# Two float16 parts for a decoder block's output and mixing products, and its scales worked out apart

## The chip, the cores and the metric

The kernel runs on one core of one Trainium2 chip. The metric is the device time of one execution in microseconds (us); lower is better. Engines are named as the profile names them: PE is TensorE (PEld its weight loads), DVE is VectorE, ACT is ScalarE, POOL is GpSimd, SP is SyncE, which issues most DMAs.

## What is computed

One decoder block on 1024 tokens of width 1024. Two token mixers work side by side on the normed input: dilated attention in three groups of eight heads, whose outputs are merged per head with softmax weights, and a causal convolution module. Their outputs are gated and added, mixed by a matrix, normed and added to the input; a SwiGLU feed-forward follows. The part that the change touches:

```python
o = jnp.einsum('gbsh,gbshd->bshd', alpha, jnp.stack(outs, axis=0))
y_attn = o.reshape(B, S, ATTN_OUT_W) @ w_attn_out              # 512 -> 1024
merged = jax.nn.sigmoid(z_ga) * y_attn + jax.nn.sigmoid(z_gc) * y_conv
x = x + rms_norm(merged @ w_mix_out, g_post_mix)               # 1024 -> 1024
h = rms_norm(x, g_pre_ffn)
x = x + rms_norm(swiglu_ffn(h, w_ffn_in, w_ffn_out), g_post_ffn)
```

## The kernel before, in words

**Products in parts.** Every large product keeps float32 accuracy with three matmuls: each operand is split into a high and a low part, and high x high, high x low and low x high are added up. Most stages use two float16 parts. Their operands are brought to a common size first by a power of two (a "scale": `peaks` or `early_scales` squares the weights on ACT with a running sum, `total` and `bound` (L142) spread the sum over the partitions by a small PE product with a block of ones (L146), and DVE makes the power of two and its inverse). Three stages use two float32r parts instead, which need no scale: the first one, the attention's output product, the mixing product (and the last, the FFN's second product).

**Order of work.** Python writes all engines' instructions in one order. `tick` (L250), called after each group of matmuls of the main loop, runs what is planned beside it: steps due at a given tick (`later`), pieces of weight splitting (one each `PIECE` ticks), and generators, of which one that yields k goes on k + 1 ticks later. Each engine then runs its own instructions in that order and waits only for data and for buffers. `slot` hands out 42 buffers of 128x1024 floats, `bank` PSUM banks by name: `g` for products, `s` (two) for small results, `t` (two) for transposes.

**The stages.** GLU (to about 190 us of the trace), gates (`gate_pair`, seven pairs, to 317), queries and keys (`qk_pair`, twelve pairs, to 530), values with the attention beside them and the rest of the attention, the convolution's output product (to 853), then

- the attention's output product (L1745 to L1759, 853 to 897): eight columns n, two halves each, and per half `unit` (L478), 4 x 3 matmuls of 128x512 (L485, L487, L489), 192 in all. DVE multiplies the result by the gate (L1753) and adds the other branch (L1754); ACT and DVE split it (L1756, L1759) into `mop`, the mixing product's operand;
- the mixing product (L1782 to L1809, 897 to 990): eight tiles of 128 tokens (the first two together), 48 matmuls of 128x512 each (L1794), 384 in all, two ticks after every six. After each tile a generator `mix_norm` (L1506) norms it; that of tile 3 and that of tile 7 also transpose four tiles' results, eight groups of four transposes (L1524) into the two `s` banks, from which ACT copies them (L1530) and splits them (L1399). It waits 9 ticks, then writes one group each 2 ticks. After a tile, L1807 runs all generators but the newest to their end at once;
- the FFN's two products (to the end), float16 in the first and float32r in the second (L2068).

**The merge** (L1319), a generator for each of four pairs of heads (its transposes start at 717 us in the first and end at 844 us in the fourth): DVE multiplies three outputs of 128x1024 by weights (L1347), adds them (L1349, L1352). Partition p holds the tokens 8p to 8p + 7, so eight 128x128 transposes (L1363, four to a bank) give every eighth token each, and ACT's copy (L1366) and DVE's low part (L1368, pairs 2 and 3 alone) put them in order with a stride. Pairs 0 and 1 go out to DRAM and come back later in `out_parts` (L1377).

**Weights of these products.** `part` (L309) splits each in two halves: ACT casts the high part (L320), DVE takes the low part of the first half and POOL that of the second (L321).

**Early scales.** `early_scales` (L191) is a generator started before the query and key pairs (L1666). For 20 weights (12 of the values, 8 of the convolution's output) it issues a load on SP (L212) and about 13 ticks later a Square on ACT with a sum (L208); after each group it works out the scale by `bound`. `input_scales` (L167) does so for two rows of gains at the start.

Of the kernel before, what the change touches and what calls it, by code (L numbers as in the profile page):

```python
# [18 lines left out]
T = 1024  # L19
# [52 lines left out]
class Build:  # L72
# [77 lines left out]

    def scales(self, i):
# [15 lines left out]
    def input_scales(self):  # L167
# [4 lines left out]
        for c in (C_PRE, C_PREF):  # L172
            m = self.tiny(2, "pk", 4)
            nc.scalar.activation(self.junk[:, :8], self.col8(c), AF.Square, scale=1 / H_TOP, accum_out=m[:, 0:1])
            p.append(self.total(m, 1))
        yield 6
        for e, c in enumerate((C_PRE, C_PREF)):
# [3 lines left out]
            self.bound(t[:, 0:1], p[e])  # L181
# [9 lines left out]
    def early_scales(self, groups):  # L191

        nc = self.nc
        m = self.small.tile([128, 24], F32, name="em")
        t = self.small.tile([128, 5], F32, name="cs")
        self.conv_bias = self.small.tile([128, 8], F32, name="cb")
        for c, x, k in ((0, C_GLN, 32), (1, C_BLN, 1)):
            nc.scalar.activation(self.junk[:, :8], self.col8(x), AF.Square, scale=k * A_TOP, accum_out=m[:, c:c + 1])
        pa = self.total(m[:, 0:2], 2)
        yield 6  # L200
        self.bound(t[:, 0:1], pa)
        nc.vector.reciprocal(t[:, 1:2], t[:, 0:1])
        yield 2
        todo = [(e, j) for e, jobs in enumerate(groups) for j in jobs]
        x, ends = None, {len(jobs) + 2 + sum(len(y) for y in groups[:e]): e for e, jobs in enumerate(groups)}
        for n in range(2, len(todo) + 3):
            if x is not None:
                nc.scalar.activation(self.junk, x, AF.Square, scale=W_TOP, accum_out=m[:, n - 1:n])  # L208
            x = None
            if n < len(todo) + 2:  # L210
                x = self.slot()
                nc.sync.dma_start(x, self.jobs[todo[n - 2][1]][0])  # L212
            yield 3
            if n in ends:
# [10 lines left out]
                for j in jobs:  # L225
                    self.scale[j] = tuple(u[:, i:i + 1] for i in range(1, 5))
            else:
                yield 8
        w = self.scale[groups[1][0]][0]
        nc.vector.tensor_tensor(t[:, 4:5], t[:, 0:1], u[:, 0:1], op=OP.mult)  # L230
        nc.vector.tensor_scalar(self.conv_bias, self.col8(C_BCO), t[:, 1:2], w, op0=OP.mult, op1=OP.mult)
        nc.vector.tensor_scalar(self.vun, self.scale[groups[0][0]][1], 1 / (KEEP * P_TOP), None, op0=OP.mult)
        self.act_scale, self.conv_un = t[:, 1:2], t[:, 4:5]
# [75 lines left out]
    def part(self, i, c):  # L309
# [7 lines left out]
        if i in self.f16:  # L317
# [1001 lines left out]
    def merge(self, hp, st, last):  # L1319
# [34 lines left out]
        yield 2 + 2 * late  # L1354
        if hp < 2:
            hi = self.slot()
        else:
            hi, lo = self.slot(F32R), self.slot(F32R)
# [825 lines left out]
```

## Time and profile before

| | us |
|---|---|
| median of 3 runs | 1618.56 (1618.04 to 1619.05) |
| the profiled execution | 1618.76 |
| its span, first to last instruction | 1616.9 |
| PE busy | 1592.5 (98%) |
| DVE busy | 1244.3 (77%) |
| ACT busy | 997.8 (62%) |
| POOL busy | 449.0 (28%) |

The granted TensorE clock is 0.999 of full speed over the span (2.4 GHz). A matmul's duration in the trace covers its whole way through the array, and the next one starts before it ends; what a stream of matmuls costs is read from the distance between starts. "Idle before" in a timeline row is the time in which the engine had nothing, and behind it stands what ended that.

### The profile page before, as it was taken

Reading aid. Unit: us, or ns where it says so; the run is one execution under the profiler, and the core shown is the slowest. Engines: PE = TensorE matmul, PEld = TensorE weight load, DVE = VectorE, ACT = ScalarE, POOL = GpSimd, SP = SyncE. Lnnn points to the kernel's source line nnn. Section 1 sums busy time; section 2 is a strip of 40 time slices with the busy share of each in tenths; the row PEclk is TensorE's granted clock in tenths of the full one; section 3 lists DMA queues with packets and bytes.
Section 4 is the critical chain, followed back from the end, with each engine's and each line's share of the span. In section 5 each row is a group of like instructions: output and inputs, shape, how many; then the busy total and the mean of one; then the engine's idle time right before and its main releaser. Section 6 shows DMA issues by size and latency. Waiting matters only on the chain.

```text
span 1616.9 us, 25346 instructions
## 1 busy us (share of the span) xinstructions
PE 1592.5 (98%) x9034; PEld 979.5 (61%) x9034; DVE 1244.3 (77%) x2415; ACT 997.8 (62%) x1900; POOL 449.0 (28%) x372
## 2 busy tenths in 40 slices
PE   8999999999999999999999999999999999999998
PEld 6744444444444799976657876444444444588886
DVE  6879999989899768787686655876656666677686
ACT  6476666778776578877752566654555454454453
POOL 0006777767777343654401200000000000000000
PEclk9999999999999999999999999999999999999999
DMA  4353333455666765777847432033322232594334
GB/s 175 109 204 110 111 135 145 145 183 201 199 180 141 223 189 159 178 224 225 253 154 278 173 115 91 27 143 111 124 99 98 108 128 91 205 335 121 134 105 156
DMA packets 158906, 254.02 MB, mean 157 GB/s; under 512 B 63313, under 2 KB 82444, under 8 KB 158780
## 3 DMA queue, kind: packets, MB, share of 16 engines
q1 hardware_dynamic: 154572, 240.23, 44.8%
q0 software_dynamic: 3920, 11.91, 2.3%
q8 instruction: 71, 1.16, 0.3%
q14 instruction: 55, 0.45, 0.1%
q10 hardware_dynamic: 288, 0.27, 0.0%
HBM read 178.52 MB, written 78.55 MB: 159 GB/s over the span
## 4 chain that ended last, share of the span: by engine, by line
PE 82%; DVE 9%; ACT 4%; issue 2%; POOL 2%; DMA 0%; DVEq 0%; SPq 0%; POOLq 0%; ACTq 0%
PE p L2068 13%; PE p L501 13%; PE p L503 13%; PE p L502 13%; PE p L485 4%; PE p L489 4%; PE p L487 4%; PE p L1794 3%; PE p L1142 2%; PE p L1144 2%; PE p L1146 2%; DVE p L885 2%; PE p L739 2%; PE p L1274 2%; PE p L1237 2%
## 5 line engine op out<-in xcount | busy, mean ns | idle before, releaser
L501 PE MATMUL p<-b,b 128*128 128x512 f16 x1032 | 390.9, 379 | 2.1 <-ACT c L515 1.6
L503 PE MATMUL p<-b,b 128*128 128x512 f16 x1032 | 391.1, 379 | 1.5 <-POOL b L340 1.5
L502 PE MATMUL p<-b,b 128*128 128x512 f16 x1032 | 391.0, 379 | 0.0
L2068 PE MATMUL p<-b,b 128*128 128x512 f32 x924 | 209.8, 389 | 0.0
L2068 PEld LDWEIGHTS p<-b,b 128*128 128x128 f32 x924 | 173.5, 188 | 36.1
L503 PEld LDWEIGHTS <-b 128*128 128x128 f16 x1032 | 100.8, 98 | 125.2 <-POOL b L340 4.0
L501 PEld LDWEIGHTS <-b 128*128 128x128 f16 x1032 | 100.9, 98 | 121.3
L502 PEld LDWEIGHTS <-b 128*128 128x128 f16 x1032 | 100.8, 98 | 119.3 <-issue 3.0
L885 DVE SCALAR_TENSOR_TENSOR p<-b,par,p 128x511 f32<-128x511 f32 (+14 forms) x232 | 164.1, 740 | 0.0
L485 PE MATMUL p<-b,b 128*128 128x512 f16 (+1 forms) x368 | 141.3, 384 | 1.6 <-ACT b L330 1.6
L489 PE MATMUL p<-b,b 128*128 128x512 f16 (+1 forms) x368 | 140.7, 382 | 0.4 <-DVE b L331 0.4
L487 PE MATMUL p<-b,b 128*128 128x512 f16 (+1 forms) x368 | 140.7, 382 | 0.0
L331 DVE SCALAR_TENSOR_TENSOR b<-d,sc,b 128x1024 f16<-128x1024 f32 x40 | 51.2, 1281 | 87.7 <-ACT b L330 87.7
L340 POOL TENSOR_TENSOR b<-d,b 128x1024 f16<-128x1024 f32 x44 | 93.9, 2134 | 83.7 <-ACT b L339 83.7
L1146 PE MATMUL p<-b,b 128*128 128x256 f16 x384 | 104.7, 273 | 0.0
L1144 PE MATMUL p<-b,b 128*128 128x256 f16 x384 | 104.7, 273 | 0.0
L1142 PE MATMUL p<-b,b 128*128 128x256 f16 x384 | 104.7, 273 | 0.0
L1399 ACT CAST b<-b 128x512 fp32r<-128x512 f32 (+1 forms) x117 | 72.1, 617 | 43.0 <-PE p L2068 18.5
L1400 DVE TENSOR_TENSOR b<-b,b 128x512 fp32r<-128x512 f32 (+1 forms) x117 | 80.1, 688 | 19.6 <-ACT b L1399 18.2
L1794 PE MATMUL p<-b,b 128*128 128x512 f32 x384 | 90.0, 392 | 0.0
L1251 ACT ACTIVATE c<-c,stat 128x128 f32<-128x128 f32 (+1 forms) x192 | 84.3, 443 | 6.8 <-DVE stat L1241 6.7
L515 ACT COPY c<-p 128x512 f32<-128x512 f32 x43 | 25.2, 585 | 100.2 <-PE p L503 64.6
(296 smaller groups left out, 3431.6 us busy)
## 6 DMA issues: line engine op xcount, KB each, us to landing
b<-w_in SPq DMA_DIRECT2D x30, 512.0 KB, 6.4
b<-w_v SPq DMA_DIRECT2D x24, 512.0 KB, 4.5
b<-w_fi SPq DMA_DIRECT2D x24, 512.0 KB, 4.4
d<-w_in SPq DMA_DIRECT2D x23, 512.0 KB, 4.3
dqS<-c SPq DMA_DIRECT2D x44, 256.0 KB, 2.0
b<-w_fo SPq DMA_DIRECT2D x44, 256.0 KB, 5.4
c<-dqS SPq DMA_DIRECT2D x44, 256.0 KB, 4.2
d<-w_fi SPq DMA_DIRECT2D x20, 512.0 KB, 3.5
```

The source lines that it names most:

```text
L485: nc.tensor.matmul(ps, hi[:, s], a, start=kt == 0, stop=False)
L487: nc.tensor.matmul(ps, hi[:, s], b, start=False, stop=False)
L489: nc.tensor.matmul(ps, lo[:, s], a, start=False, stop=kt == nk - 1)
L501: nc.tensor.matmul(ps, hi[:, s], a, start=first and kt == 0, stop=False, skip_group_check=True)
L502: nc.tensor.matmul(ps, hi[:, s], b, start=False, stop=False, skip_group_check=True)
L503: nc.tensor.matmul(ps, lo[:, s], a, start=False, stop=kt == 3, skip_group_check=True)
L885: nc.vector.scalar_tensor_tensor(A[i][:, j:], src[i][:, :H - j], w[i], A[i][:, j:], op0=OP.mult, op1=OP.add)
L1142: nc.tensor.matmul(o, a, hi[:, s], start=kt == 0, stop=False)
L1144: nc.tensor.matmul(o, a, lo[:, s], start=False, stop=False)
L1146: nc.tensor.matmul(o, b, hi[:, s], start=False, stop=kt == KT - 1)
L1794: nc.tensor.matmul(banks[tt][nh], st, wt[:, nh * H:(nh + 1) * H], start=bool(kt == 0 and a), stop=bool(kt == KT - 1 and b))
L2068: nc.tensor.matmul(acc[t], x, y, start=first and e == 0, stop=last and e == 2, skip_group_check=True)
```

## The change

- Output and mixing products get two float16 parts: `B.f16` takes in the jobs `ao` (8 weights of 512 columns) and `mx` (8 of 1024), `mop` is packed float16, and `both` gives float16 parts for pairs 0 and 1. Their scales come from `early_scales`, now for 36 weights (16 more loads and Squares), with one job each 12 ticks, started before the gate pairs.
- The size of the merged attention output is measured: one Square with a sum on ACT per merge, and a new generator `mix_scales` after the fourth.
- `root` takes the place of `bound` for gains and for that sum: a PE transpose of one column, spread to 128, and a DVE maximum along the row. `largest` prepares the gains' column. Small DVE operations that stood together are spread by yields.
- The merge's transposes: for each half of the partitions (64 rows), eight transposes of 64x128 into every eighth column of a bank, so 16 a merge, with the result in token order.
- The weights `ao` and the first two of `mx` are brought to size by ACT first (`pre`), and POOL takes all their low parts; the other six of `mx` go by `scaled_parts` (ACT and DVE).
- In the output product the high part of a half is taken one half later, the low part two halves later.
- `mix_norm` of tile 3 writes one group of transposes each 3 ticks.

The diff, cut to its core:

```diff
+    def root(self, a, m):
+        ps = self.bank(self.stag)
+        nc.tensor.transpose(ps[:, :128], m.to_broadcast([128, 128]), self.ident)
+        nc.vector.tensor_reduce(a, ps[:, :128], AX.X, OP.max)
...
     def early_scales(self, groups):
...
             if n < len(todo):
                 x = self.slot()
-                nc.sync.dma_start(x, self.jobs[todo[n - 2][1]][0])
+                src, k, _ = self.jobs[todo[n][1]]
+                nc.sync.dma_start(x[:, :k], src)
             yield 3
...
             else:
-                yield 8
+                yield 7
...
+    def mix_scales(self):
+        yield 4
+        nc.vector.tensor_reduce(r, self.osq[:, :4], AX.X, OP.add)
+        yield 4
+        self.root(on, r)
...
-        if i in self.f16:
+        if i in self.pre:
+            if c == 0:
+                nc.scalar.activation(r[:, :n], r[:, :n], AF.Copy, scale=self.scale[i][0])
+            nc.scalar.copy(hi[:, s], r[:, s])
+            nc.gpsimd.tensor_tensor(lo[:, s], r[:, s], hi[:, s], op=OP.subtract)
+        elif i in self.f16:
...
-        yield 2 + 2 * late
+        yield 2
+        nc.scalar.activation(self.junk, O[0], AF.Square, scale=self.o_scale, accum_out=self.osq[:, hp:hp + 1])
...
+        yield 1 + 2 * late
...
         for h in range(2):
             ps = self.bank("t")
-            for i in range(4):
-                u = h * 4 + i
-                nc.tensor.transpose(ps[:, i * 128:(i + 1) * 128], O[0][:, u * 128:(u + 1) * 128], self.ident)
+            r = slice(h * 64, h * 64 + 64)
+            for u in range(8):
+                nc.tensor.transpose(ps.rearrange("p (m u) -> p u m", u=8)[:, u], O[0][r, u * 128:(u + 1) * 128],
+                                    self.ident[r, r])
...
-            self.OT[hp] = self.both(x)
+            self.OT[hp] = self.both(x, self.o_scale, True)
...
-                yield 1
+                yield 1 + (tt == 3)
...
-    B.f16 = {*range(glu_jobs[3][0], ao[0]), *range(B.fi0, len(J))}
-    B.early = [i for p in vj.values() for i in p] + co
-    B.pre = {*range(glu_pairs[0] - 1, min(vj[0, 0]))}
+    B.f16 = {*range(glu_jobs[3][0], len(J))}
+    B.early = [i for p in vj.values() for i in p] + co + ao + mx
+    B.pre = {*range(glu_pairs[0] - 1, min(vj[0, 0])), *ao, *mx[:2]}
...
+    es = B.bg(B.early_scales((B.early[:12], co, ao, mx)))
     for n in range(4):
         B.gate_pair(B.d_ga[2 * n:2 * n + 2], ga[n])
...
-    es = B.bg(B.early_scales((B.early[:12], co)))
...
-            nc.vector.tensor_tensor(c[:, s], ps, c[:, s], op=OP.mult)
+            nc.vector.scalar_tensor_tensor(c[:, s], ps, B.att_un, c[:, s], op0=OP.mult, op1=OP.mult)
...
+            x = mop[hf][n] = B.packed()
+            todo.append((x, c[:, s]))
+            if len(todo) > 1:
+                high(*todo[-2])
+            if len(todo) > 2:
+                low(*todo.popleft())
```

## Rows read from the trace of the kernel before

**Rows 1.** The page: busy time of each engine, its share of the span, instructions.

```profile
PE 1592.5 (98%) x9034; PEld 979.5 (61%) x9034; DVE 1244.3 (77%) x2415; ACT 997.8 (62%) x1900; POOL 449.0 (28%) x372
```

**Rows 2.** Windows: length, busy time by engine, clock; gates, queries and keys, output product.

```profile
190.00:317.00 127.00, 126.70 (x593) 57.32 (x592) 121.38 (x199) 87.80 (x132) 94.99 (x62) 1.00 0.39 141
317.00:530.00 213.00, 212.25 (x996) 95.94 (x994) 187.32 (x347) 161.47 (x266) 158.01 (x101) 1.00 0.61 182
853.10:896.80 43.70, 43.70 (x194) 36.21 (x193) 34.17 (x53) 14.46 (x30) 7.08 (x8) 1.00 0.78 274
```

**Rows 3.** Waits of PE: who, for whom, us in total, times, longest.

```profile
PE p L1524 <- ACT b L1530: 1.4, 1, 1.4
PE p L1363 <- DVE c L1287: 0.9, 1, 0.9
```

**Rows 4.** Timeline of PE, output product (start, duration): first and last of 28 rows.

```profile
859.68 0.39 PE L487 MATMUL p<-b,b 128*128 128x512 f32 x1
...
865.80 0.39 PE L487 MATMUL p<-b,b 128*128 128x512 f32 x1
```

**Rows 5.** Timeline of PE, gate pairs: first and last of 48 rows.

```profile
299.82 0.38 PE L501 MATMUL p<-b,b 128*128 128x512 f16 x1
...
309.96 0.38 PE L503 MATMUL p<-b,b 128*128 128x512 f16 x1
```

**Rows 6.** Timeline of PE, mixing product, its sixth tile with the transposes of L1524.

```profile
960.91 1.64 PE L1794 MATMUL p<-b,b 128*128 128x512 f32 x6
962.39 0.60 PE L1524 MATMUL p<-ident,b 128*128 128x128 f32 x4
962.74 1.64 PE L1794 MATMUL p<-b,b 128*128 128x512 f32 x6
965.79 0.66 PE L1524 MATMUL p<-ident,b 128*128 128x128 f32 x4 [1.41 <-ACT b L1530]
```

**Rows 7.** Timeline of ACT in the same tile.

```profile
962.89 1.15 ACT L1516 ACTIVATE b<-d,rr 128x1024 f32<-128x1024 f32 x1 [0.87 <-DVE rr L1484]
...
965.07 0.68 ACT L1530 ACTIVATE b<-p,hg 128x512 f32<-128x512 f32 x1
```

**Rows 8.** Timeline of PE, a merge's transposes between two products.

```profile
721.15 0.60 PE L1363 MATMUL p<-ident,b 128*128 128x128 f32 x4
721.58 0.38 PE L485 MATMUL p<-b,b 128*128 128x512 f16 x1
```

**Rows 9.** Timeline of PE at the start: matmuls of one float32 column.

```profile
33.03 1.84 PE L582 MATMUL p<-mean_col,b 128*128 128x1 f32 x16
```

**Rows 10.** Weight loads by line: shortest, median, longest ns; first and last start.

```profile
L582 PEld LDWEIGHTS p<-mean_col,b x32: 188/192/192, 32.8 to 572.5; 128*128 128x128 f32 x32
L1363 PEld LDWEIGHTS p<-ident,b x32: 139/141/143, 717.4 to 844.0; 128*128 128x128 f32 x32
```

**Rows 11.** Timeline of PE: a product of 33 rows and 8 columns among full ones.

```profile
71.70 0.47 PE L485 MATMUL p<-b,b 128*128 128x512 f32 x1
72.01 0.39 PE L487 MATMUL p<-b,b 128*128 128x512 f32 x1
72.24 0.40 PE L489 MATMUL p<-b,b 128*128 128x512 f32 x1
72.57 0.81 PE L642 MATMUL p<-b,tab 33*8 33x384 f32 x2
73.31 0.50 PE L485 MATMUL p<-b,b 128*128 128x512 f32 x1
```

**Rows 12.** Timeline of PE: transposes of a spread column.

```profile
578.53 1.04 PE L597 MATMUL p<-ident,rs 128*128 128x128 f32 x8
```

**Rows 13.** Single lines: shortest, median, longest ns; first and last start; shapes.

```profile
L1754 DVE SCALAR_TENSOR_TENSOR b<-b,cs,b x16: 750/752/1129, 857.0 to 898.7; 128x512 f32<-128x512 f32 x16
L208 ACT ACTIVATE junk<-b x20: 1039/1052/1066, 331.3 to 493.4; 128x1024 bf16<-128x1024 f32 x20
```

**Rows 14.** Timeline of DVE: the merge's last addition.

```profile
714.09 1.21 DVE L1352 TENSOR_TENSOR b<-b,b 128x1024 f32<-128x1024 f32 x1
```

More of the change, by code (lines that the diff above doesn't have):

```diff
@@ L180, in input_scales @@
             t = self.small.tile([128, 5], F32, name=f"hs{e}")
-            self.bound(t[:, 0:1], p[e])
+            self.root(t[:, 0:1], p[e])
             nc.vector.reciprocal(t[:, 1:2], t[:, 0:1])
@@ L226, in early_scales @@
                     self.scale[j] = tuple(u[:, i:i + 1] for i in range(1, 5))
+                uns.append(u)
             else:
-                yield 8
[L229 to L233, printed above, removed]
+                yield 7
@@ new lines, in early_scales @@
+        self.mix_w = mu
+        self.mix_scale, self.mix_un, self.mix_root = (t[:, i:i + 1] for i in range(8, 11))
+        self.osq = self.small.tile([128, 8], F32, name="osq")
+    def mix_scales(self):
+        nc = self.nc
+        r, on = self.osq[:, 4:5], self.osq[:, 5:6]
+        yield 4
+        nc.vector.tensor_reduce(r, self.osq[:, :4], AX.X, OP.add)
+        yield 4
+        self.root(on, r)
+        y = self.mix_un
+        nc.vector.scalar_tensor_tensor(y, on, self.att_top, self.conv_top, op0=OP.mult, op1=OP.add)
+        self.power(y, y)
+        nc.vector.tensor_scalar(y, y, 2.0 ** -14, TINY, op0=OP.mult, op1=OP.max)
+        nc.vector.reciprocal(self.mix_scale, y)
+        nc.vector.tensor_tensor(y, y, self.mix_w, op=OP.mult)
+        nc.vector.tensor_scalar(self.mix_root, y, ROOT, None, op0=OP.mult)
@@ L1491, in residual @@
         for nh in range(2):
-            nc.scalar.activation(out[:, nh * H:(nh + 1) * H], banks[nh], AF.Square, scale=ROOT, accum_out=ss[:, nh:nh + 1])
+            nc.scalar.activation(out[:, nh * H:(nh + 1) * H], banks[nh], AF.Square, scale=self.mix_root, accum_out=ss[:, nh:nh + 1])
         yield gap
@@ L1740, in build, with high, low @@
     mop = [[None] * 8, [None] * 8]
-    rest = lambda: None
+    todo = deque()
+    def high(x, c):
+        nc.scalar.activation(x[:, :H], c, AF.Copy, scale=B.mix_scale)
+    def low(x, c):
+        nc.vector.scalar_tensor_tensor(x[:, H:], c, B.mix_scale, x[:, :H], op0=OP.mult, op1=OP.subtract)
     B.PIECE = 1
@@ L1752, in build @@
             ps = B.unit(w, lambda kt: tuple(x[:, s] for x in B.OT[kt]), 4)
-            nc.vector.tensor_tensor(c[:, s], ps, c[:, s], op=OP.mult)
+            nc.vector.scalar_tensor_tensor(c[:, s], ps, B.att_un, c[:, s], op0=OP.mult, op1=OP.mult)
             nc.vector.scalar_tensor_tensor(c[:, s], y[:, s], B.conv_un, c[:, s], op0=OP.mult, op1=OP.add)
-            x = B.slot(F32R)
-            nc.scalar.copy(x[:, :H], c[:, s])
-            mop[hf][n] = x
-            rest()
-            rest = lambda x=x, c=c[:, s]: nc.vector.tensor_tensor(x[:, H:], c, f(x[:, :H]), op=OP.subtract)
-    y = None
-    rest()
+            x = mop[hf][n] = B.packed()
[4 more added lines that the diff above has]
+                low(*todo.popleft())
+    high(*todo[-1])
+    while todo:
+        low(*todo.popleft())
+    x = y = None
     B.OT = None
+    assert B.mixing not in B.gens
     W = [B.weights(mx[0])]
```

79 lines of the change are left out of this document (59 added, 20 removed).

## The prediction

> **What bounds the kernel now.** First the page's busy times: PE works 1592.5 of 1616.9 us, no other engine over 77% [rows 1]. An average can hide stages, so the windows come next: in the gates, in the queries and keys and in the output product PE is busy for all but 0.3, 0.75 and 0 us, at full clock (1.00), while DVE, the next engine, has 121 of 127 us in the gates and 34 of 44 in the output product [rows 2]. Last PE's waits: of those near the change the longest is 1.4 us, on ACT's copy of transposed columns in the mixing product, and 0.9 in a merge [rows 3]. So a change moves the time only by what PE has to run and by the stalls that it adds or takes from PE; work on ACT, DVE, POOL and SP is free as long as PE does not come to wait for it.
>
> **Parts in float16: the gain.** In the output product 27 steps from start to start take 865.80 - 859.68 = 6.12 us, 0.2267 each, with float32r parts [rows 4]; in the gates, with float16 and the same 128x512 shape, 47 steps take 10.14 us, 0.2157 each [rows 5]. The difference is 0.0110 us. It meets 192 matmuls of the output product and 384 of the mixing product: 576 x 0.0110 = **-6.3 us**. The number of products stays three, so nothing else goes from PE.
>
> **The transposes of tile 3.** They stand among the sixth tile's products. Now the seventh group waits 1.41 us [rows 6] because ACT is late: its queue stood 0.87 us for DVE before L1516, and the copy that frees the bank starts at 965.07 only [rows 7]. With 16 ticks a tile, the groups come at ticks 18, 20, ... 32 after tile 3, and the generator is run to its end at tick 32. With one group each 3 ticks they come at 18, 21, 24, 27, 30, and three are left, which are then written one behind the other after the tile. PE waits less inside the tile and more at its end, since there are two banks and ACT's queue holds the same work in the same order. I take the tile to end when ACT lets it, as now: then the faster products gain nothing in it, 48 x 0.011 = **+0.5**. Ends: -1.4 if the wait goes and no other comes; +2.5 if all three last groups wait for ACT. For that a group costs ACT 0.68 for the copy [rows 7] and about as much for the split's high part, so some 1.3 x 3 = 3.9, less the 1.4 of now.
>
> **The merges' transposes.** Four full ones take 721.58 - 721.15 = 0.43, 0.107 each [rows 8], so 32 take 3.4 us. After it 64 have half the columns to stream. Lower end: half the time each, 64 x 0.054 = 3.4, no change. Upper end: a load of 128 columns of weights sets the pace, as where 16 products with one column follow at (1.84 - 0.25)/15 = 0.106 [rows 9] (0.25 is one's duration, an estimate from how long the last outlasts its start): 64 x 0.106 = 6.8, +3.4. But that was a plain float32 load, of 192 ns; a transpose's takes 141 [rows 10], 0.051 shorter, which leaves a pace of about 0.055 to 0.06. I take 0.06: **+0.4**.
>
> These transposes use 64 of the array's rows, then full products follow, on eight visits (four merges, two halves). The nearest row is a product of 33 rows: before it 72.24 to 72.57 is 0.33 where 0.227 is usual, 0.10 lost; after it L485 starts late too, but the 0.31 from 71.70 to 72.01 stands without such a neighbour [rows 11], so I charge 0.10 a visit: **+0.8**. Ends 0 and 0.33 a visit, +2.6: a full drain in and out, each the 0.38 that a product lasts less the 0.216 to the next start [rows 5].
>
> The Trainium skill ("TensorEngine Tiling (Array Packing)", Key Properties) states that a change of tiling mode drains TensorE. By that rule this term would be the upper end, 2.6, and the sum 1.8 higher; the 0.10 lost before the product of 33 rows is less than such a drain.
>
> **Scales on PE.** Five of `root`'s transposes at 0.11 (eight take 1.04, with 0.27 for the last one's way through [rows 12]) and four products of `bound` stand where five of the latter stood: 5 x 0.11 less next to nothing, **+0.5**. Ends: 0.3, and 2 if one of them waits for a late DVE in the gates.
>
> **What lies beside PE.** Costed at nothing, each with its cover:
> - Early scales: 36 loads and Squares, one each 12 ticks, from the first gate pair. A Square is 1.05 us [rows 13] and its read-out some 0.2; in the gates' 127 us about 16 come, 20 us on top of ACT's 88 [rows 2]. That is 85%, against 76% in the queries and keys, where the Squares ran already and PE lost 0.75 in 213 us. DVE, at 96% in the gates, gets a dozen small operations. If this cover goes, ACT's copies of the accumulators come late and PE waits for the bank at the next product.
> - SP: 16 more loads, 6 MB, queued behind the gates' stores, at a DMA share of 0.39 and 0.61 [rows 2]. A load has 12 ticks, 7.8 us; a late one holds ACT's queue at its Square.
> - Output product: DVE's three steps on a half become three of 0.75 [rows 13], 2.25 us in the 12 x 0.2157 = 2.59 that PE needs, and lose their share of the weights' splitting. POOL, busy 7 of 44 us there [rows 2], takes that. High and low parts come one and two halves later: the last low parts of the first token half end some 3 us into the mixing product, which needs that column last, about 18 us in.
> - The merges: ACT gets a Square of 128x1024 each and copies without a stride; DVE's low part is shorter.
> - The new wait: `mix_scales` holds a PE transpose behind DVE's sum of four Squares, five ticks (3.2 us) after it; behind it queue the convolution's last products.
>
> **Sum.** -6.3 + 0.5 + 0.4 + 0.8 + 0.5 = -4.1. The profiled execution took 1618.76 us, its span and 1.9 around it; that gives 1614.7. The median of the runs is 0.2 lower: **1614.5 us**.
>
> **Rivals.**
> 1. *More is gained.* PE's wait in the sixth tile goes (-1.4 where I have +0.5) and the half transposes cost nothing (0 where I have 0.4 + 0.8): 1614.5 - 1.9 - 1.2 = 1611.4. For it: three ticks a group are more time for ACT inside the tile. Against: the burst at its end.
> 2. *PE gives it back in the transposes.* The load of 128 columns sets their pace: +3.0, 1617.5; with full drains as well +1.8, 1619.3. For it: the pace of 0.106 whatever streams [rows 9]. Against: the shorter load of a transpose [rows 10]. The Trainium skill ("TensorE: Matmul & The Clock Gate", LDWEIGHTS) has a load last by its columns alone, rows not counting, columns over 1.2 GHz: 128 columns would be 107 ns and this rival true. No run here shows a transpose's load set the pace.
> 3. *Another engine becomes the bound in the output product.* DVE's longer steps hold each of 16 halves at the present 12 x 0.2267 = 2.72 us: 16 x 0.13 = +2.1, 1616.6. Against: 2.25 us of DVE work a half.
> 4. *Slower: ACT's queue stands behind the merges' Squares.* Each waits for L1352 (1.21 us [rows 14]) and runs 1.05; what follows in ACT's order, the attention's exponentials and copies, comes late, and PE already waits in a merge [rows 3]. If all of it reaches PE: 4 x 2.26 = 9.0, 1623.5. It makes the kernel slower once more than 1.8 of the 2.26 us reach PE in each merge ((4.1 + 3.2)/4). Against: a transposed block is used two steps of the attention after ACT's copy.
>
> **How the numbers follow.** A measurement of this kernel can tell about 0.2%, 3.2 us, from no change: under 1615.3 is faster, over 1621.8 slower. Chances: my forecast 0.50, rival 1 0.16, rival 2 0.18, rival 3 0.08, rival 4 0.08. The forecast's own range, 1612.5 to 1616.5, lies for five sixths under 1615.3, 0.42; with rival 1 that is 0.58 for faster, 0.08 for slower, 0.34 for no difference. The range reaches from rival 1 to rival 2 without the drains and a little past them, 1611.2 to 1618.2; left out are rival 4, the drains of rival 2 and the tails.
>
> **What would show it.** Right: starts 0.216 apart in the output and mixing products, these stages together 6 us shorter, 64 transposes at about 0.06, the sixth tile as long as now with its wait at the end. Wrong: transposes at 0.107; starts of 0.3 or more around them; PE waits for ACT in the gates or the merges; halves of the output product that keep 2.7 us.

## The result, and the profile after

The kernel became slower: 1626.65 us (median of 6 runs, 1626.07 to 1627.13) against 1618.80 (6 runs, 1618.04 to 1619.40) of the kernel before beside it, a ratio of 1.0049, 95% interval 1.0036 to 1.0061. The forecast was 1614.5, its range ended at 1618.2. The profiled execution took 1626.69 us, its span is 1624.6.

The page's busy times, which answer to [rows 1]: PE is again at 98%, and no other engine has come over 77%. As before, this row can't show where 7.7 us went.

```profile
PE 1591.7 (98%) x9070; PEld 930.4 (57%) x9070; DVE 1255.5 (77%) x2455; ACT 1022.4 (63%) x1946; POOL 453.5 (28%) x377
```

So the span is cut where a stage's first matmul starts. In this table each column is the time from there to the next stage's first matmul, in us; the lines below the second are the experiments that follow, and the last column is the median of a run's times. The stages are those of one profiled execution, which lay up to 2.7 us above its run's median (e5) and 1.6 below it (e4), so they need not add up to it. What is left out moves by under 0.3 us between all of them, apart from the start (112.8 to 114.5, whatever the kernel).

| run | gates | queries, keys | values, late gate | conv output | output product | mixing | plain products | median |
|---|---|---|---|---|---|---|---|---|
| before | 127.7 | 219.2 | 197.8 | 119.6 | 43.7 | 93.1 | 45.0 | 1618.8 |
| after | 129.6 | 222.5 | 198.6 | 121.7 | 41.4 | 95.4 | 45.0 | 1626.7 |
| e1 no spacing | 129.6 | 222.5 | 198.6 | 121.7 | 41.4 | 92.5 | 45.7 | 1626.0 |
| e2 late transposes | 129.6 | 222.5 | 200.2 | 121.7 | 41.4 | 91.2 | 47.1 | 1625.7 |
| e5 short chain | 129.6 | 222.5 | 200.1 | 121.7 | 41.4 | 94.5 | 45.0 | 1625.6 |
| e6 mixing order | 129.6 | 222.5 | 200.2 | 121.7 | 41.4 | 86.5 | 46.5 | 1619.9 |
| e3 one bank more | 129.6 | 221.2 | 198.6 | 121.7 | 41.4 | 93.9 | 45.2 | 1625.3 |
| e7 scales by DMA | 129.1 | 223.6 | 200.2 | 121.7 | 41.4 | 95.2 | 45.0 | 1629.3 |
| e9 bank phase | 128.3 | 220.6 | 198.6 | 121.8 | 41.4 | 95.1 | 45.0 | 1623.2 |
| e12 fewer squares | 129.6 | 221.0 | 200.2 | 121.7 | 41.4 | 93.9 | 45.2 | 1626.0 |
| e14 phase, fewer squares | 128.3 | 218.6 | 198.6 | 121.7 | 41.4 | 95.1 | 45.2 | 1621.6 |
| e4 full transposes | 129.6 | 222.5 | 199.1 | 127.2 | 41.4 | 95.0 | 45.0 | 1634.9 |
| e8 both | 130.0 | 226.2 | 198.6 | 121.7 | 41.4 | 86.5 | 46.5 | 1622.1 |
| e10 phase and order | 128.3 | 220.7 | 198.6 | 121.8 | 41.4 | 86.5 | 47.2 | 1617.1 |
| e11 first merges full | 128.3 | 220.6 | 198.8 | 121.3 | 41.4 | 86.5 | 47.2 | 1616.6 |
| e13 eighth as before | 128.3 | 220.7 | 198.8 | 121.3 | 41.4 | 86.5 | 46.4 | 1616.3 |

After against before: gates +1.9, queries and keys +3.3, late gate +0.8, conv output +2.2, output product -2.3, mixing +2.3; with -0.5 at the start that is the +7.7 of the span.

The windows of after (length, busy time and instructions by engine, clock, DMA share, GB/s) answer to [rows 2]: gates, queries and keys, output product, mixing, and two short stretches inside the mixing.

```profile
188.40:318.00 129.60, 127.99 (x599) 57.80 (x598) 123.73 (x214) 102.94 (x164) 96.06 (x62) 1.00 0.56 199
318.00:540.50 222.50, 218.43 (x1024) 98.92 (x1023) 199.39 (x364) 163.45 (x272) 157.95 (x101) 1.00 0.60 175
860.80:902.20 41.40, 41.40 (x193) 18.75 (x192) 35.83 (x44) 22.84 (x39) 16.90 (x16) 1.00 0.97 379
902.20:997.60 95.40, 90.36 (x421) 42.04 (x420) 57.22 (x162) 57.76 (x114) 0.22 (x1) 0.96 0.20 69
...
958.60:961.80 3.20, 2.97 (x8) 1.25 (x9) 1.07 (x7) 3.20 (x9) 0.00 (x0) 0.50 0.24 85
...
975.70:978.90 3.20, 3.20 (x9) 1.13 (x8) 1.86 (x4) 3.14 (x7) 0.00 (x0) 0.50 0.00 0
```

The output product keeps PE full, as hoped. The gates, the queries and keys and the mixing now have 1.6, 4.1 and 5.0 us without work on PE, and in the mixing the granted clock is 0.50 (1.2 GHz) twice. Who is waited for says the waits view of PE (us in total, times, longest), first of gates to keys, then of the mixing; they answer to [rows 3].

```profile
PE p L1203 <- DVE c L1098: 2.1, 1, 2.1
PE p L562 <- ACT c L576: 1.3, 1, 1.3
PE p L562 <- DVE c L1046: 1.2, 1, 1.2
PE p L562 <- DVE c L1098: 0.7, 1, 0.7
PE p L155 <- DVE pm L170: 0.3, 1, 0.3
```

```profile
PE p L1597 <- ACT b L1589: 2.9, 1, 2.9
PE p L1597 <- ACT b L1603: 2.1, 2, 1.1
```

L1597 is the fourth tile's transposes (L1524 before), L1589 the Copy that ends a tile's norm (L1516), L1603 the copy out of PSUM (L1530), L1564 the squares of a tile's product (L1492), L562 the Winograd products (L501), L1203 the first product of the values (L1142), L1098 and L1046 DVE's last step on a key, query or gate. An experiment's own rows have lines shifted by its edit. The experiments' texts place the waits by time and count them from start to start of two products, less the usual 0.216: there the 1.2, 1.3 and 0.7 of this view are 1.4 at 204.6, 1.5 at 432 and 0.85 at 501.

### The profile page after: what moved, and what is told of

Its sections match the earlier page's. It is cut to its first block, busy times and chain, and to the rows that moved or that the text cites. A ratio compares the mean times of both kernels' runs of the same rounds, so it can differ in the third digit from the quotient of the medians.

```text
span 1624.6 us, 25507 instructions
## 1 busy us (share of the span) xinstructions
PE 1591.7 (98%) x9070; PEld 930.4 (57%) x9070; DVE 1255.5 (77%) x2455; ACT 1022.4 (63%) x1946; POOL 453.5 (28%) x377
## 4 chain that ended last, share of the span: by engine, by line
PE 80%; DVE 10%; ACT 5%; issue 2%; POOL 2%; DMA 1%; DVEq 0%; SPq 0%; ACTq 0%; POOLq 0%
PE p L2152 13%; PE p L562 12%; PE p L564 12%; PE p L563 12%; PE p L546 4%; PE p L550 4%; PE p L548 4%; DVE p L946 3%; PE p L1878 3%; PE p L1203 2%; PE p L1205 2%; PE p L1207 2%; PE p L800 2%; PE p L1335 2%; PE p L1298 2%
## 5 line engine op out<-in xcount | busy, mean ns | idle before, releaser
L562 PE MATMUL p<-b,b 128*128 128x512 f16 x1032 | 391.0, 379 | 3.5 <-ACT c L576 2.9
L564 PE MATMUL p<-b,b 128*128 128x512 f16 x1032 | 391.1, 379 | 1.1 <-POOL b L401 1.1
L563 PE MATMUL p<-b,b 128*128 128x512 f16 x1032 | 391.1, 379 | 0.0
L2152 PE MATMUL p<-b,b 128*128 128x512 f32 x924 | 209.8, 389 | 0.0
L562 PEld LDWEIGHTS <-b 128*128 128x128 f16 x1032 | 101.0, 98 | 121.1
L401 POOL TENSOR_TENSOR b<-d,b 128x1024 f16<-128x1024 f32 x44 | 93.9, 2134 | 84.2 <-ACT b L400 84.2
L1203 PE MATMUL p<-b,b 128*128 128x256 f16 x384 | 104.7, 273 | 2.1 <-DVE c L1098 2.1
L1878 PE MATMUL p<-b,b 128*128 128x512 f16 x384 | 87.2, 389 | 0.0
L576 ACT COPY c<-p 128x512 f32<-128x512 f32 x43 | 25.2, 585 | 92.6 <-PE p L564 58.4
```

What stands on the lines that cost most here:

```text
L562: nc.tensor.matmul(ps, hi[:, s], a, start=first and kt == 0, stop=False, skip_group_check=True)
L563: nc.tensor.matmul(ps, hi[:, s], b, start=False, stop=False, skip_group_check=True)
L564: nc.tensor.matmul(ps, lo[:, s], a, start=False, stop=kt == 3, skip_group_check=True)
L1203: nc.tensor.matmul(o, a, hi[:, s], start=kt == 0, stop=False)
L1878: nc.tensor.matmul(banks[tt][nh], st, wt[:, nh * H:(nh + 1) * H], start=bool(kt == 0 and a), stop=bool(kt == KT - 1 and b))
L2152: nc.tensor.matmul(acc[t], x, y, start=first and e == 0, stop=last and e == 2, skip_group_check=True)
```

## Experiments on the mixing

The timeline of PE around the first wait of the mixing, and ACT's in the same stretch (start, duration):

```profile
954.55 1.03 PE L1878 MATMUL p<-b,b 128*128 128x512 f16 x4
955.41 0.49 PE L1597 MATMUL p<-ident,b 128*128 128x128 f32 x3
958.83 0.47 PE L1597 MATMUL p<-ident,b 128*128 128x128 f32 x1 [2.93 <-ACT b L1589]
```

```profile
948.77 1.15 ACT L1589 ACTIVATE b<-d,rr 128x1024 f32<-128x1024 f32 x1 [0.87 <-DVE rr L1556]
949.83 0.67 ACT L1564 ACTIVATE d<-p,cs 128x512 f32<-128x512 f32 x1
...
955.29 1.06 ACT L1587 ACTIVATE b<-d 128x1024 f32<-128x1024 f32 x1 [3.71 <-DVE d L1576]
...
957.63 1.15 ACT L1589 ACTIVATE b<-d,rr 128x1024 f32<-128x1024 f32 x1 [0.87 <-DVE rr L1556]
```

ACT goes through one tile's norm after another: the third tile's Copy starts at 948.77, only behind it the fourth tile's squares, at 957.63 its Copy, 8.86 us a tile. PE has three blocks of the first group and stands until the fourth tile's is there. **Theory A**: this chain, in both kernels about 56 us from the mixing's start to the fourth Copy's end, is what sets the transposes; the faster products just come to them sooner, 53 us in. In the kernel before, PE came to them 56 us in, just as that Copy ended (PE, then ACT):

```profile
953.23 0.60 PE L1524 MATMUL p<-ident,b 128*128 128x128 f32 x4
```

```profile
952.09 1.15 ACT L1516 ACTIVATE b<-d,rr 128x1024 f32<-128x1024 f32 x1 [0.87 <-DVE rr L1484]
```

**e1_no_spacing.**

```diff
-                yield 1 + (tt == 3)
+                yield 1
```

> The fourth tile's transposes come one tick apart as before, not two; nothing else differs from the kernel after. Theory A (the norm's chain of 56 us from the mixing's start is the bound, and the faster products reach the transposes before it ends): the wait of 2.9 us on the Copy of L1589 stays, with one stretch of 3.4 us at half clock behind it; the two waits of 1.0 on L1603 and the second half-clock stretch go, one wait of 1.4 on L1603 as in [rows 6] comes back. Mixing falls from 95.4 to about 93.0 us, the kernel by 2.4 to about 1624.2. Rival (the wider spacing is what costs, and the first wait follows from it): the first wait goes too, mixing falls to about 88.5 and the kernel by 7 to about 1619.7.

The wait on the Copy stayed at 3.0 us, one wait of 1.2 on the copies was left, and one half-clock stretch of 3.41 us. Mixing 92.5, plain products +0.7: -2.3 for both together, as theory A said; the rival falls. The median moved by 0.6 only; in the profiled execution the start alone took 1.5 us more than in that of after.

**e2_late_transposes.** (Extract; buffers are also let go earlier.)

```diff
-            yield 8
+            yield 14 if tt == 3 else 8
...
-            for e in norms[:-1]:
+            for e in norms[:-2]:
```

> The fourth tile's transposes start six ticks (3.9 us by 0.65 a tick) later, and the loop no longer forces that tile's norm to its end with the next tile; the wider spacing stays. Theory A (chain of the norm): no wait over 0.3 us on L1589 or L1603 in the mixing, no half-clock stretch; 384 products at 0.2157 are 82.8, 32 transposes at 0.109 are 3.5, so mixing takes 86.3 to 88 us instead of 95.4; the kernel falls by about 7.5 to 1619. Rival (the vector and scalar engines' work on the tiles is the limit, whenever the transposes come): new waits in the sixth to eighth tile, mixing 91 to 95, the kernel falls by at most 4.

A miss for theory A as it stood; the times are those of the rival. The first three groups came in time, but the fourth found its bank, the second group's, still full and waited 2.9 us. ACT's timeline shows why (L1605 is the copy out of PSUM here, L1588 and L1590 the fifth tile's norm):

```profile
963.08 0.67 ACT L1605 ACTIVATE b<-p,hg 128x512 f32<-128x512 f32 x1
966.38 1.06 ACT L1588 ACTIVATE b<-d 128x1024 f32<-128x1024 f32 x1 [2.63 <-DVE d L1576]
...
968.73 1.15 ACT L1590 ACTIVATE b<-d,rr 128x1024 f32<-128x1024 f32 x1 [0.87 <-DVE rr L1556]
...
970.90 0.68 ACT L1605 ACTIVATE b<-p,hg 128x512 f32<-128x512 f32 x1
```

The second group's transposes ended near 964.4, and their copy came at 970.90: in ACT's order it stands behind the fifth tile's norm, which waits for DVE. The Trainium skill ("TensorE: Matmul & The Clock Gate", Part 1) has ACT's and DVE's queues strictly first in, first out; these rows agree. So the transposes need two things, the fourth norm done and a gap in ACT's order. Mixing and plain products together fell by 2.2 us.

**e5_short_chain.** In `residual` and `mix_scales`:

```diff
-            ... AF.Square, scale=self.mix_root, accum_out=ss[:, nh:nh + 1])
+            ... AF.Square, scale=ROOT, accum_out=ss[:, nh:nh + 1])
-        nc.vector.tensor_scalar(ss[:, 2:3], ss[:, 0:1], RMS_EPS, None, op0=OP.add)
+        nc.vector.tensor_scalar(ss[:, 2:3], ss[:, 0:1], self.mix_root, None, op0=OP.add)
-        nc.vector.tensor_tensor(r, r, self.mix_un, op=OP.mult)
...
-        nc.vector.tensor_scalar(self.mix_root, y, ROOT, None, op0=OP.mult)
+        nc.vector.reciprocal(e, y)          # e is self.mix_root
+        nc.vector.scalar_tensor_tensor(e, e, RMS_EPS, e, op0=OP.mult, op1=OP.mult)
```

> The norm of a mixing tile goes back to the operations it had before the change: the squares take a constant instead of a column as scale (the squares on ACT took 0.59 before and 0.67 after), and the product with the column of unscales on DVE (0.16, one more step of 0.19) goes; the column is put into the small number under the root instead, once for all tiles, which gives the same result. The transposes stay where they are. Theory A (serial chain of four norms, 37.1 us after the change and 35.9 before it, sets the fourth tile's transposes): the chain is back at about 35.9, the first wait falls from 2.9 to about 1.8 us, mixing by 1.2 or, if the shorter wait no longer brings a half-clock stretch, by up to 2.9; the kernel 1623.8 to 1625.5. Rival E (the chain has slack elsewhere, the wait comes from the waiting for the row's transfers or the split's pieces): the wait stays at 2.9 and the kernel within 0.5 of after.

The first wait fell from 2.9 to 1.6 us, as theory A has it: the change had made each norm longer by itself. But the later waits grew from 2.1 to 2.8 us, and among them the granted clock fell to half for 6.83 us in this execution, so mixing fell by 0.9 only.

**e6_mixing_order.** e5's edit, and:

```diff
-        yield 1
+        banks = x = None
+        yield 14 if tt == 4 else 1
         hn = self.slot()
...
-            yield 8
+            x2 = None
+            yield 13 if tt == 3 else 10
...
-                yield 1 + (tt == 3)
+                yield 1
...
-            for e in norms[:-1]:
+            for e in norms[:-2]:
```

> The short chain, the fourth tile's transposes five ticks later and one tick closer together, the fifth tile's own norm (square, root, copy) held 13 ticks back so that ACT's queue is free for the transposes' copies, the eighth tile's transposes two ticks later, and no forced end of the fourth norm with the sixth tile. Theory A (chain, and ACT's queue in program order behind it, as the run with late transposes showed): no wait over 0.5 us and no half-clock stretch in the mixing; 82.8 + 3.5 and small change, 86.5 to 88 us instead of 95.4, the plain products behind it 45.0 to 45.7; the kernel falls by about 7 to 1619.5. Rival (ACT and DVE are full, the waits only move): mixing and plain products together fall by less than 4 us.

The windows of this run: a stretch behind the hand-over to the values, then the mixing and the plain products.

```profile
542.10:545.30 3.20, 3.20 (x17) 2.28 (x16) 0.00 (x0) 0.00 (x0) 0.00 (x0) 0.50 1.06 298
904.10:990.60 86.50, 86.50 (x422) 41.41 (x421) 55.19 (x151) 55.33 (x112) 0.23 (x1) 1.00 0.19 64
990.60:1037.10 46.50, 45.37 (x227) 22.52 (x226) 29.97 (x60) 34.28 (x56) 0.00 (x0) 1.00 0.19 65
```

Mixing 86.5, every microsecond of it busy at full clock: 82.8 for the products and 3.5 for the transposes. The plain products took 1.5 more, since PE now comes to the eighth tile's transposes while ACT is late with their copies. The ratio to before is 1.0009 (1.0000 to 1.0017). ACT and DVE have nearly the same work here (55 us each, 58 and 57 after), so e2's rival falls too. So the mixing's loss is explained: of 95.4 us after, 86.5 is work, 3.3 the halved clock (16 steps of up to 0.427 us where 0.216 is usual) and the other 5.6 the waits.

## Experiments on the early scales

The hand-over from keys to values, after: PE's last key product and first value product, then DVE's last step on a key. Behind them the first value product and DVE's last step before the change.

```profile
538.02 0.38 PE L564 MATMUL p<-b,c 128*128 128x512 f16 x1
540.48 0.27 PE L1203 MATMUL p<-b,b 128*128 128x256 f16 x1 [2.09 <-DVE c L1098]
539.74 0.69 DVE L1098 SCALAR_TENSOR_TENSOR c<-p,c 128x512 f16<-128x512 f32 x1 [1.84 <-ACT c L1097]
```

```profile
535.81 0.27 PE L1142 MATMUL p<-b,b 128*128 128x256 f16 x1
537.32 0.69 DVE L1037 SCALAR_TENSOR_TENSOR c<-p,c 128x512 f16<-128x512 f32 x1 [1.84 <-ACT c L1036]
```

PE waits until DVE has read the last product. Before, PE went on at once though DVE's step came equally late. Which of five banks a product gets is fixed when the kernel is built, and every scale formed by PE takes one too. **Theory B**: six scales instead of three shift this order, so that the first value product gets the bank of the last key product, and at other places a product gets a bank that was read late. **Rival C**: ACT's and DVE's added work makes them late.

**e3_one_bank_more.** At the end of `early_scales`:

```diff
+        self.root(t[:, 11:12], pb)
+        yield 4
```

> One more reduction of the same kind (a transpose into one of the five banks, three small operations into a spare column) at the very end of the early scales; all their other work is the same. Theory B (the order in which the five banks are handed out: the last key product and the first value product take the same bank, so PE waits for the last L1098): now the last product takes another bank, and the wait of 2.1 us at the hand-over goes, the other waits of the queries and keys (1.7 and 1.1 us) stay; queries and keys 222.5 to 220.3, the kernel down by 2.1 to about 1624.5. Rival C (the vector engine has too much to do with the small operations and the squares): the hand-over's wait stays at 2.1 or grows, and the kernel gains 0 to 0.5.

The hand-over's wait fell from 2.1 to 0.7 and is for another reader (ACT's copy in the running sum), the other two stayed, as B says; queries and keys gave 1.3 instead of 2.1.

**e7_scales_by_dma.** `root` and `bound` replaced for the six scales (extract):

```diff
+        nc.sync.dma_start(d, m)
+        yield 8
+        w = self.slot()[:, :128]
+        nc.sync.dma_start(w, bass.AP(tensor=s.tensor, offset=s.offset, ap=[[0, 128], [1, 128]]))
+        yield 8
+        nc.vector.tensor_reduce(a, w, AX.X, op)
```

> The six early scales are formed without TensorE and without one of the five banks: a column goes to memory and comes back as a 128 by 128 tile, and DVE reduces that; all squares, loads and small operations stay, and 12 small transfers and six reductions of 128 columns from SBUF come on top. The mixing is as after. Theory B (banks: each scale takes one of five banks out of turn, and holds it until DVE comes to it): the waits of 1.4 us at 204.6, 1.5 at 432 and 0.85 at 501 and the scales' own transposes go, the hand-over to the values takes another bank (0 to 0.8); gates 129.6 to about 127.3, queries and keys 222.5 to 218.5 to 219.5, the kernel down by 4.5 to 6 to about 1621.3. Rival C (load on ACT and DVE): gates and queries together fall by less than 1.5, and waits on DVE's or ACT's lines come at other places.

Inconclusive. The waits named went, but others came. In the waits of ACT the gates' and keys' own weights are now late (0.9 us in all after the change), and SP's queue stood 28 us for the landing of the small transfers, with the loads behind them:

```profile
ACT junk L131 <- DMA d<-w_in: 15.3, 6, 4.2
```

**e9_bank_phase.** Moments alone, the squares' too:

```diff
-        yield 6
+        yield 31
         self.root(t[:, 0:1], pa)
...
-        yield 6
+        yield 23
         self.root(t[:, 2:3], pb)
-        yield 4
+        yield 5
...
-                yield 1
+                yield 2
                 p = self.total(r, 1)
...
-                yield 7
+                yield 5
```

> Only the moments differ: the six early scales take their bank three ticks behind the pair's own scale, before the pair's third product takes one; the same operations, the same number of banks, and the loads and squares even two ticks closer together. The last product before the values then lies in another bank than the first value product. Theory B (bank order): the waits of 1.4 us at 204.6, 1.5 at 432, 0.85 at 501 and 2.1 at the hand-over go; gates 129.6 to about 127.8, queries and keys 222.5 to 218 to 219; the kernel down by 5 to 6 to about 1621, and no half-clock stretch behind the hand-over. Rival C (load of the squares and small operations): with the load denser the waits stay or grow, gates and queries together fall by less than 1.5 us.

All four waits of over 0.5 us that the waits view of after shows went, but new ones of up to 0.8 us came: gates and queries together -3.2, where B had 5 or more and C under 1.5. Median 1623.2, ratio 1.0028 (1.0019 to 1.0038). So 3.2 of 5.2 us hang on the moments, but not all of that on banks. The wait of 1.2 in the gates is for the same DVE step as in the kernel before, where it ended as PE came to the product, which lost 0.3 us (before, then after):

```profile
204.40 0.68 DVE L985 TENSOR_TENSOR c<-p,c 128x512 f32<-128x512 f32 x1
205.14 0.38 PE L501 MATMUL p<-b,c 128*128 128x512 f16 x1
```

```profile
205.44 0.68 DVE L1046 TENSOR_TENSOR c<-p,c 128x512 f32<-128x512 f32 x1
206.18 0.38 PE L562 MATMUL p<-b,c 128*128 128x512 f16 x1 [1.21 <-DVE c L1046]
```

After, ten small DVE steps of the scales, 1.6 us in all, stand ahead of it from 193.65 on; in e9 only three of them. For the wait of 1.3 ACT's copy L576 came late, because the scale's own small copy L139 stood ahead of it and waited for DVE's sum:

```profile
432.91 0.19 ACT L139 CAST pb<-er 128x1 bf16<-128x1 f32 x1 [3.11 <-DVE er L241]
433.01 0.58 ACT L576 COPY c<-p 128x512 f32<-128x512 f32 x1
```

Before, the product there hung on the same copy, which came in time (429.54). The reader of the 0.7 wait, L1098 at 501.22, came behind six small steps on DVE (from 499.09); whether its bank changed as well is open. B in its own sense, another bank, is shown for the hand-over alone.

**e12_fewer_squares.**

```diff
-            if n < len(todo):
+            if n < len(todo) and todo[n][0] < 2:
                 x = self.slot()
...
-                nc.vector.tensor_reduce(r, m[:, n - len(jobs):n], AX.X, OP.add)
+                nc.vector.tensor_reduce(r, m[:, (n if n <= 20 else 20) - len(jobs):n if n <= 20 else 20], AX.X, OP.add)
```

> The early scales as after, same ticks, banks and small operations, but without the 16 loads and 16 squares of the output and mixing weights: these two groups take the conv output weights' sum in place of their own. Theory B (bank order): the waits at 204.6, 432, 501 and the hand-over stay within 0.3 us each, gates and queries 129.6 and 222.5; the kernel as after within 1 us. Rival C (load): gates and queries fall by 2 or more, the kernel to about 1624 or less.

Between the theories: the waits at 204.6 and the hand-over stayed, that at 501 went and that at 432 fell from 1.5 to 0.9; together -1.5.

**e14_phase_fewer_squares.** Both edits.

> The moments of the bank-phase run together with the missing 16 loads and squares; the two groups again take the conv output weights' sum. If bank order and load each have their own share: gates 127.9 to 128.3, queries and keys 220.6 - 1.5 = 219.1 or less, the kernel about 1621.7. If they are the same microseconds (the squares only shifted one scale's wait): 128.3 and 220.4 to 220.7, the kernel as the bank-phase run, 1623.2.

Windows of gates and of queries and keys, then all waits of PE in them:

```profile
189.30:317.60 128.30, 127.67 (x599) 57.90 (x598) 123.44 (x210) 100.84 (x161) 95.77 (x62) 1.00 0.55 193
317.60:536.20 218.60, 218.10 (x1025) 98.96 (x1024) 196.09 (x367) 151.59 (x241) 158.18 (x101) 1.00 0.53 150
```

```profile
PE p L564 <- POOL b L401: 0.5, 1, 0.5
PE p L562 <- DVE p L1110: 0.5, 1, 0.5
```

346.9 us for both stages, what before took. Each has its share: 3.2 for the moments, and 2.0 more for 16 loads and squares. ACT has 151.6 us to do here instead of 163.5; an engine 73% busy still made PE wait where its order put a square ahead of a copy (in e9 the waits for copies at 411 and 475 us, 0.8 and 0.6, which are gone here). Loads and squares went together; which of them counts was not taken apart.

## The merges, and the parts together

A merge's half transposes after (start, duration), which answer to [rows 8]:

```profile
728.79 0.19 PE L1366 MATMUL p<-b,c 128*128 128x64 f16 x1
728.92 0.71 PE L1430 MATMUL p<-ident,b 64*128 64x64 f32 x8
729.56 0.39 PE L546 MATMUL p<-b,b 128*128 128x512 f16 x1
```

Of eight transposes the second starts 0.11 us behind the first and the others 0.063 apart (0.71 less the last one's 0.22 is 0.49 for seven steps). Into them 0.13 passes where 0.03 is usual (0.10 lost), the second step loses 0.05, and out of them 0.155 passes where 0.063 would do (0.09 lost): 0.24 a visit, in all eight. The next texts reckon with 0.19, without the second step.

**e4_full_transposes.** In the merge:

```diff
-            for u in range(8):
-                nc.tensor.transpose(ps.rearrange("p (m u) -> p u m", u=8)[:, u], O[0][r, ...], self.ident[r, r])
-            a = hi[:, h * H:(h + 1) * H]
+            for i in range(4):
+                nc.tensor.transpose(ps[:, i * 128:(i + 1) * 128], O[0][:, ...], self.ident)
+            y = ps.rearrange("p (u m) -> p u m", u=4)
+            a = hi.rearrange("p (m u) -> p u m", u=8)[:, h * 4:h * 4 + 4]
...
-                nc.vector.scalar_tensor_tensor(lo[:, h * H:(h + 1) * H], y, self.o_scale, a,
+                nc.vector.scalar_tensor_tensor(lo.rearrange("p (m u) -> p u m", u=8)[:, h * 4:h * 4 + 4], y, self.o_scale, a,
```

> The merges' transposes are full 128 by 128 ones again (32 instead of 64), read out of PSUM with strides as before; the scale, the float16 parts and the squares stay. Theory D (row switching at 0.19 us a visit and 64 half transposes at 0.063 against 32 at 0.109): 8 x 0.19 + 64 x 0.063 - 32 x 0.109 = 2.0; the conv output's stage falls from 121.7 to 119.7, the kernel by 2.0 to about 1624.6. Rival (the stage's extra 2.2 us are the squares and scaled parts on the scalar and vector engines, which hold the transposes' banks): 0 to 0.5 gained, and the waits on L1348 and around the merges stay.

Both were wrong: 8.3 us slower. The lines of this run for the high and low part, which write float16 with a step of eight elements:

```profile
L1435 DVE SCALAR_TENSOR_TENSOR b<-p,cs,b 128x512 f16<-128x512 f32 x4 | 10.0, 2502 | 3.7 <-ACT b L1434 3.7
...
L1434 ACT ACTIVATE b<-p,cs 128x512 f16<-128x512 f32 x4 | 10.2, 2543 | 1.7 <-PE p L1430 1.5 <-issue 0.2
```

The same after, without a step:

```profile
L1435 ACT ACTIVATE b<-p,cs 128x512 f16<-128x512 f32 x4 | 2.7, 687 | 5.9 <-PE p L1430 4.0 <-issue 1.9
L1436 DVE SCALAR_TENSOR_TENSOR b<-p,cs,b 128x512 f16<-128x512 f32 x3 | 2.2, 746 | 1.2 <-ACT b L1435 1.2
```

DVE came to its next steps late by these, and PE waited for them at the end of the conv output, 6.6 us in three waits:

```profile
PE p L546 <- DVE b L1799: 3.3, 1, 3.3
PE p L546 <- DVE osq L156: 1.7, 1, 1.7
PE p L155 <- DVE osq L280: 1.6, 1, 1.6
```

Without those the stage took 127.2 - 6.6 = 120.6, 1.1 less than after: that is the sign of theory D, not its 2.0. Token order in PSUM is what makes float16 parts affordable here.

**e8_both** (e6 and e7):

> The two edits together (order of the mixing's norms, early scales without banks). If both theories hold, the gains add: 1626.7 - 7 - 5.3 = about 1614.4, 4 us under the kernel before; what is then left of the change's costs is the merges' half transposes (about 2). If one gain is taken back by the other's side (later loads, other bank order), 1617 or more.

Mixing 86.5, but 226.2 for queries and keys: e7's late loads, this time with a half-clock stretch. The second case of the text (1622.1).

**e10_phase_and_order** (e9 and e6, the eighth tile's `yield` 12):

> That edit with the mixing's edit (short chain, transposes where ACT's queue is free), the eighth tile's transposes two more ticks later. If theories A and B hold, the gains add: mixing 86.5, plain products 45 to 46, gates and queries about 5 us less; 1626.7 - 5.5 - 8 = about 1613, 5 to 6 us under the kernel before. If bank order and load can't be had apart (rival C), 1617 to 1620.

1617.1 us, ratio 0.9994 (0.9985 to 1.0003). Every stage has the value it had alone, but for the plain products, 47.2. That is the second case of the text, 4 us above the first, of which e9 alone had missed 2.

**e11_first_merges_full.** For `hp < 2` the four full transposes and the strided float32 copy of before.

> The same, and the first two of four merges, whose result stays float32, go back to four full transposes a half and a strided copy. Theory D (each visit to the 64-row mode costs 0.19 us, and 16 half transposes at 0.063 are 0.14 more than 8 full ones at 0.109): 4 x 0.19 + 2 x 0.14 = 1.0 us less in the stages of the late gate and the conv output (22.3 + 121.7 after), the kernel about 1612. Rival (strided copies on ACT, 1.09 against 0.69 us, come back as waits, as in the run with all full transposes): no gain, or up to 1 us lost.

Conv output -0.5, late gate +0.25; 1616.6, ratio 0.9988 (0.9979 to 0.9997). A quarter of what D had in all: the pair in the conv output gave its half, but in the late gate the waits grew by 0.5, 0.3 of it for the strided copy.

**e13_eighth_as_before** (e11, the eighth tile's `yield` 8 again):

> The run before this with the eighth tile's transposes back where they were after the change (four ticks earlier); all else the same. Theory F (the later transposes put their copies behind the scalar engine's table load and Silu of the plain products: waits of 0.99 and 0.86 us on L1609): the two waits go, the plain products fall from 47.2 to 45.0 to 45.7, the kernel from 1616.6 to about 1614.8, clearly under the kernel before. Rival (the eighth norm itself is late, as PE comes to it sooner now): a wait on the eighth norm's copy of 0.5 to 1.5 us takes their place, and the plain products stay above 46.5.

Plain products 46.4, between the two: one wait of 1.0 on the copies stays. 1616.3 us against 1618.5 beside it, ratio 0.9986 (0.9977 to 0.9995): the fastest version with e11 (1616.6), 10 us under the change as made and 2 under before. Its windows, mixing and plain products:

```profile
899.10:985.50 86.40, 86.40 (x421) 41.38 (x420) 55.14 (x150) 55.30 (x111) 0.18 (x1) 1.00 0.18 64
985.50:1031.90 46.40, 45.40 (x226) 22.52 (x225) 29.84 (x59) 34.30 (x57) 0.00 (x0) 1.00 0.19 65
```

## Why the prediction was wrong

- **"Parts in float16: the gain", -6.3: right as a price.** In the output product 33 steps are 0.2157 each (first and last row below), and the stage lost 2.3 us where 192 x 0.011 has 2.1. The mixing's 4.2 was there to be had (e6), and was lost again in the next point.

```profile
867.68 0.38 PE L550 MATMUL p<-b,b 128*128 128x512 f16 x1
...
874.80 0.38 PE L550 MATMUL p<-b,b 128*128 128x512 f16 x1
```

- **"The transposes of tile 3", +0.5 with ends at -1.4 and +2.5: the step that failed most.** The stage came out 6.0 us over what this and the gain had for it. "I take the tile to end when ACT lets it" looked at the copies of one tile [rows 6, 7]. What bound was four norms one behind the other in ACT's order, and PE came to their end with nothing to spare already before: the faster a tile's products, the longer the wait (2.9 us, which the text did not have at all). The change also lengthened that chain (squares 0.67 us against 0.58 to 0.59 with a constant, one more DVE step): e5 without this has 1.6 of the 2.9 left. The rows of the fourth norm were not read. The burst at the end came as described (two waits of 1.05 us).
- **The clock: no term.** At the end of these waits and behind them the granted clock stood at 0.50 for 3.41 us at a time, and 128x512 products started 0.427 apart: 3.3 us in the mixing of after. The Trainium skill ("TensorE: Matmul & The Clock Gate", Part 1) has these two states and says that idle time brings the lower one; the rows agree in that each stretch stands at or behind waits, but not each wait has one. A stall of PE has to be priced with it.
- **"Early scales ... costed at nothing": the second failure, 5.2 us** (with 0.3 of it for two transposes that had a term). The sentence on the cover named the very wait ("PE waits for the bank at the next product"), but gave it neither a price nor a rival, with DVE at 121 of 127 us in [rows 2]; only "Scales on PE" had an end of 2, for a late DVE in the gates. What runs here costs by its moment (3.2: what stands ahead of a bank's reader in DVE's and ACT's order, and at the hand-over which bank) and by its load (2.0).
- **"The merges' transposes": +0.4 right, +0.8 too low.** The pace is 0.063 where 0.06 was taken. Row switching costs 0.10 on the way in, as charged, 0.05 at the second transpose, and 0.09 on the way out, which was read as free: 1.9 in eight visits. All makes 8 x 0.24 + 64 x 0.063 - 32 x 0.109 = 2.5 of the 3.0 that late gate and conv output lost; 0.2 more are longer waits in these stages, and 0.3 was not taken apart.
- **The rules weighed.** A full drain in and out was priced at 0.33 a visit; 0.24 was measured. The Trainium skill ("TensorEngine Tiling (Array Packing)", Key Properties) states that a change of tiling mode drains TensorE; the rows show a loss on the way in and out, but less than two full drains by that price. A load of 128 columns as the pace was priced at 0.106 a transpose; 0.063 was measured, so rival 2 is out for the pace. The Trainium skill ("TensorE: Matmul & The Clock Gate", LDWEIGHTS) has a load's time go by its columns; that this time sets the pace of such transposes, the rows don't show.
- **Rivals.** Rival 3 fell (output product 41.4, PE without a gap), rival 4 has no wait to its name behind a merge's Square. The slower side was given 0.08, by one mechanism that didn't happen; the two that did had no chance of their own.

## What to carry to other kernels

Before a product is made faster, find what its consumer waits for: if a chain on other engines already ends just as PE arrives, the gain comes back as a wait, and perhaps as a lower clock behind it. "Beside PE" is a price of zero only if the moment is checked too: which PSUM bank a small helper takes out of turn, who reads it, and what stands ahead of that reader in its engine's order. A helper's own small steps count too: they push back whatever stands behind them in that engine's order. Moving six such helpers, by 4 to 28 us, was worth more here (3.2 us) than the whole gain in the output product.

## What the hardware did that was not expected

- The clock went to half at the end of PE's waits or just behind them, but the same wait did not always bring it: the 2.1 us at the hand-over brought a stretch of 3.41 us in e2, e6 and e12 (values and late gate 200.2 instead of 198.6) and none in the profiled execution of after. Two waits of under 0.8 us in the late gate, which after and most other runs have too, brought one in e5 and e7 alone (200.1 and 200.2).
- Writing float16 out of PSUM with a step of eight elements took 2.5 us for 128x512 on ACT and DVE alike, without a step 0.69 and 0.75; float32 with the same step took 1.09 on ACT, without 0.58.
- A scale given as a column instead of a constant made ACT's Square of 128x512 0.09 us longer (0.677 against 0.588).
